# Layer norm with residual: 16-row loads and stores as two transfers of 64 partitions

## The chip, the cores and the metric

The kernel runs on one core of one Trainium2 chip. The metric is the device time of one execution in microseconds (us), lower is better. The kernel before takes 243.0 us (median of 3 runs, 242.81 to 243.03).

For one core, a run is called slow when it is more than 1.5% above the fastest run of the same kernel. Ratios below are the mean time of one kernel's fast runs over the mean of the fast runs of the other kernel in the same rounds, so they are not quite the ratio of the medians quoted beside them.

## The reference

```python
batch, seq, dim = 16, 1024, 512          # x and residual: float32, 33.6 MB each
z = x + residual
mean = np.mean(z, axis=-1, keepdims=True)
var = np.var(z, axis=-1, keepdims=True)
return gamma * (z - mean) / np.sqrt(var + eps) + beta
```

It is a stream: 67.1 MB come in, 33.6 MB go out, and each element sees little arithmetic. The whole kernel is a question of how 100.7 MB are moved.

## The kernel before

The 16384 rows are taken as 128 rows for each of 128 partitions. A block is 16 rows a partition, and 16 rows of one partition lie together in device memory (32 KB). Loads take 8 rows at a time (16 KB a partition, 2 MB in all), stores 16 rows (32 KB a partition, 4 MB). All of them go down one queue from SyncE, over 128 partitions.

```python
BLOCK = 16
X_CHUNKS = [8] * 15 + [4, 4]
R_CHUNKS = [8] * 15 + [4, 4]
OUT_CHUNKS = [16] * 7 + [8, 4, 4]
Z_ROWS = 64        # x, z and the result share this ring: 64 rows
R_ROWS = 32        # ring for the residual: 32 rows
STORE_LAG = 40     # a store is asked for 40 rows after its rows were
# ...
    def load_x(lo, n):
        nc.sync.dma_start(out=part(zbuf, Z_ROWS, lo, n), in_=dram(xf, lo, n))

    def load_r(lo, n):
        nc.sync.dma_start(out=part(rbuf, R_ROWS, lo, n), in_=dram(rf, lo, n))

    def store(lo, n):
        nc.sync.dma_start(out=dram(of, lo, n), in_=part(zbuf, Z_ROWS, lo, n))
# ... add (GpSimd), statistics (ScalarE), two affine steps (VectorE) ...
    for lo, n in spans(X_CHUNKS):
        asked = lo + n
        load_x(lo, n)                    # waits until the ring's old rows are stored
        while loads_r and loads_r[0][0] + loads_r[0][1] <= asked:
            # ... compute until the ring's old rows are added
            load_r(*loads_r.pop(0))
        store_due()                      # stores whose last row is <= asked - STORE_LAG
```

Of the kernel before, what the change touches and what calls it, by code (L numbers as in the profile page):

```python
# [12 lines left out]
BLOCK = 16  # L13


X_CHUNKS = [8] * 15 + [4, 4]
R_CHUNKS = [8] * 15 + [4, 4]
OUT_CHUNKS = [16] * 7 + [8, 4, 4]

GROUP = 4  # L20
# [1 line left out]
Z_ROWS = 64  # L22
R_ROWS = 32
# [5 lines left out]
def kernel(  # L29
# [9 lines left out]
    nc = tc.nc  # L39
    P = nc.NUM_PARTITIONS  # L40
    xf = x.flatten_outer_dims()
    rf = residual.flatten_outer_dims()
    of = out.flatten_outer_dims()
# [4 lines left out]
    def spans(sizes):  # L48

        assert sum(sizes) == total  # L50
        return [(sum(sizes[:c]), n) for c, n in enumerate(sizes)]
# [3 lines left out]
    def dram(t, lo, n):  # L55

        k = lo % BLOCK
        assert k + n <= BLOCK
        v = t[P * (lo - k) : P * (lo - k + BLOCK), :].rearrange("(p j) d -> p j d", p=P)
        return v[:, k : k + n, :].rearrange("p a b -> p (a b)")  # L60
# [15 lines left out]
    zbuf = consts.tile([P, Z_ROWS, D], FP32)  # L76
    rbuf = consts.tile([P, R_ROWS, D], FP32)

    def part(buf, size, lo, n):
        assert lo % size + n <= size  # L80
        return buf[:, lo % size : lo % size + n, :].rearrange("p a b -> p (a b)")

    def load_x(lo, n):
        nc.sync.dma_start(out=part(zbuf, Z_ROWS, lo, n), in_=dram(xf, lo, n))  # L84

    def load_r(lo, n):
        nc.sync.dma_start(out=part(rbuf, R_ROWS, lo, n), in_=dram(rf, lo, n))  # L87

    def store(lo, n):
        nc.sync.dma_start(out=dram(of, lo, n), in_=part(zbuf, Z_ROWS, lo, n))  # L90

    def zrow(j):
        return zbuf[:, j % Z_ROWS, :]
# [16 lines left out]
    groups = []  # L110
    for lo, n in spans(R_CHUNKS):
        for j in range(0, n, GROUP):
# [92 lines left out]
    added = done = asked = 0  # L205
    loads_r = spans(R_CHUNKS)
    stores = spans(OUT_CHUNKS)

    def store_due():
        nonlocal added, done  # L210
        while stores and (
            stores[0][0] + stores[0][1] <= asked - STORE_LAG or asked == total
        ):
            lo, n = stores.pop(0)
            while done < lo + n:
                added, done = next(steps)
            store(lo, n)

    for lo, n in spans(X_CHUNKS):
        asked = lo + n  # L220
        assert not stores or stores[0][0] >= asked - Z_ROWS
        load_x(lo, n)
        while loads_r and loads_r[0][0] + loads_r[0][1] <= asked:

            while added < loads_r[0][0] + loads_r[0][1] - R_ROWS:
                added, done = next(steps)
            load_r(*loads_r.pop(0))
        if lo == 0:
            spread()
        store_due()  # L230
# [35 lines left out]
```

## Time and profile before

| what | before |
|---|---|
| time | 243.0 us |
| span of the profile | 241.3 us |
| share of the data queue in the span of 16 engines | 97.9% |
| VectorE, ScalarE, GpSimd busy | 178.5, 180.1, 144.3 us |
| transfers | 44 |

From the page of the kernel before: the span, the busy share of the DMA engines in tenths and their rate in 40 slices, the data queue (packets, MB, share), the residual add on GpSimd, and the issues (KB each, median us from issue to landing).

```profile
span 241.3 us, 1109 instructions
...
DMA  7999999999999999999999999999999999999992
GB/s 261 434 435 434 434 430 418 421 425 432 432 470 436 391 426 421 429 434 426 430 434 437 430 424 429 429 451 410 425 426 432 475 387 418 462 434 432 413 410 117
DMA packets 6349, 100.74 MB, mean 417 GB/s; under 512 B 706, under 2 KB 706, under 8 KB 708
...
q1 hardware_dynamic: 6336, 100.67, 97.9%
...
L120 POOL TENSOR_TENSOR zbuf<-zbuf,rbuf 128x2048 f32<-128x2048 f32 x32 | 144.1, 4526 | 70.6 <-DMA rbuf<-in_residual_dram 69.6
...
zbuf<-in_x_dram SPq DMA_DIRECT2D x15, 2048.0 KB, 29.2
...
out_dram<-zbuf SPq DMA_DIRECT2D x7, 4096.0 KB, 28.6
```

The engines that move data are busy in every slice but the first and the last, and the rate stands at about 430 GB/s. No compute engine is busy for more than three quarters of the span. The kernel is bound by its transfers.

The small packets (706 under 512 B) are read here as completion records: 16 for each of 44 transfers, and one each for gamma and beta, make 706. Sixteen records are taken to mean that a transfer was spread over all 16 engines, which goes with the DMA share of 1.02 of 16 engines in both stretches below.

Two stretches from the windows view of the same trace. The columns are the stretch, its length, the busy time of PE, PEld, DVE, ACT and POOL (with counts), the clock, the DMA share and GB/s.

```profile
5.00:13.00 8.00, 2.07 (x2) 0.50 (x2) 0.00 (x0) 0.00 (x0) 0.02 (x1) 1.00 1.02 434
60.00:80.00 20.00, 0.00 (x0) 0.00 (x0) 19.86 (x34) 19.87 (x61) 17.95 (x5) 1.00 1.02 437
```

The trace also holds every packet with its start and its duration. A 16 KB packet takes 612 ns and a 32 KB packet 1213 ns (medians). That is 26.8 and 27.0 GB/s for each engine, and 16 such engines make about 430 GB/s.

### The profile page before, as it was taken

The page shows a single profiled execution, that of the slowest core. Times are in us where ns is not written, and L with a number is a line of the kernel's source. Part 1 is how long each engine was busy: PE and PEld are TensorE (multiplying, and loading weights), DVE is VectorE, ACT ScalarE, POOL GpSimd, SP SyncE. Part 2 cuts the span into 40 slices and gives each one's busy share as a digit, 9 for nine tenths or more (in the row PEclk, how much of TensorE's full clock was granted, in tenths as well). Part 3 has the DMA queues.
Part 4 walks back from the last instruction along what each step waited for, and adds up shares of the span by engine and source line. Part 5 has one row for each costly group of instructions (what it writes and reads, how often), then busy time and mean ns, then how long its engine had stood idle before and what let it go on. Part 6 is the DMA issues. An engine that isn't in the chain of part 4 may idle for free.

```text
span 241.3 us, 1109 instructions
## 1 busy us (share of the span) xinstructions
PE 4.1 (2%) x4; PEld 1.0 (0%) x4; DVE 178.5 (74%) x290; ACT 180.1 (75%) x546; POOL 144.3 (60%) x36
## 2 busy tenths in 40 slices
PE   3300000000000000000000000000000000000000
PEld 0000000000000000000000000000000000000000
DVE  0005999999999999899934999359991699969200
ACT  2009999999999999999709997099961999697000
POOL 0088988989889507894078940889209891860000
DMA  7999999999999999999999999999999999999992
GB/s 261 434 435 434 434 430 418 421 425 432 432 470 436 391 426 421 429 434 426 430 434 437 430 424 429 429 451 410 425 426 432 475 387 418 462 434 432 413 410 117
DMA packets 6349, 100.74 MB, mean 417 GB/s; under 512 B 706, under 2 KB 706, under 8 KB 708
## 3 DMA queue, kind: packets, MB, share of 16 engines
q1 hardware_dynamic: 6336, 100.67, 97.9%
q14 instruction: 9, 0.07, 0.1%
q10 hardware_dynamic: 4, 0.00, 0.0%
HBM read 67.11 MB, written 33.55 MB: 417 GB/s over the span
## 4 chain that ended last, share of the span: by engine, by line
DMA 62%; ACT 16%; DVE 6%; POOL 6%; SPq 1%; issue 1%; DVEq 0%; POOLq 0%
DMA rbuf<-in_residual_dram 34%; DMA out_dram<-zbuf 28%; ACT junk L131 9%; ACT junk L140 7%; POOL zbuf L120 6%; DVE zbuf L175 3%; DVE zbuf L161 3%; SPq L84 1%; ACT std L148 0%; SPq L87 0%; SPq L90 0%; DVEq L261 0%; DVE rstd L173 0%; POOLq L120 0%; DVEq L161 0%
## 5 line engine op out<-in xcount | busy, mean ns | idle before, releaser
L120 POOL TENSOR_TENSOR zbuf<-zbuf,rbuf 128x2048 f32<-128x2048 f32 x32 | 144.1, 4526 | 70.6 <-DMA rbuf<-in_residual_dram 69.6
L161 DVE SCALAR_TENSOR_TENSOR zbuf<-zbuf,nm,gamma_t 128x512 f32<-128x512 f32 x128 | 89.5, 746 | 44.4 <-issue 22.5
L131 ACT ACTIVATE junk<-zbuf 128x512 f32<-128x512 f32 x128 | 74.2, 580 | 38.9 <-POOL zbuf L120 38.9
L175 DVE SCALAR_TENSOR_TENSOR zbuf<-zbuf,rstd,beta_t 128x512 f32<-128x512 f32 x128 | 87.1, 743 | 1.2
L140 ACT ACTIVATE junk<-zbuf,nm 128x512 f32<-128x512 f32 x128 | 85.9, 671 | 0.0
L140 ACT ACTIVATION_READ_ACCUMULATOR junk<-zbuf,nm 128x1 f32 x128 | 24.0, 187 | 0.0
L131 ACT ACTIVATION_READ_ACCUMULATOR junk<-zbuf 128x1 f32 x128 | 23.9, 187 | 0.0
L148 ACT ACTIVATE std<-ssq,eps_t 128x4 f32<-128x4 f32 x32 | 8.5, 267 | 1.0
L173 DVE RECIPROCAL rstd<-std 128x4 f32<-128x4 f32 x32 | 5.6, 175 | 0.0
L186 ACT ACT_TABLE_LOAD x1 | 1.3, 1283 | 1.5 <-PEq L247 1.5
L190 PE MATMUL beta_t<-gb_row,ones 1*128 1x512 f32 x2 | 2.1, 1136 | 2.3 <-DMA gb_row<-in_beta_dram 2.3
L190 PE MATMUL gamma_t<-gb_row,ones 1*128 1x512 f32 x2 | 2.0, 1122 | 2.3 <-DMA gb_row<-in_gamma_dram 2.3
L104 DVE MEMSET ones<- 1x128 f32 x1 | 0.2, 165 | 0.8 <-PEq L247 0.8
L190 PEld LDWEIGHTS beta_t<-gb_row,ones 1*128 1x128 f32 x2 | 0.5, 308 | 3.9 <-DMA gb_row<-in_beta_dram 3.9
L190 PEld LDWEIGHTS gamma_t<-gb_row,ones 1*128 1x128 f32 x2 | 0.5, 308 | 2.2 <-issue 2.2
L247 POOL MEMSET const-float32-0.0<- 128x1 f32 x1 | 0.1, 99 | 0.2 <-issue 0.2
L186 ACT ACTIVATE warm<-eps_t 128x1 f32<-128x1 f32 x1 | 0.2, 203 | 0.0
L247 POOL MEMSET const-bfloat16-1.0<- 128x1 bf16 x1 | 0.1, 102 | 0.0
L247 POOL MEMSET const-uint8-127<- 128x1 uint8 x1 | 0.1, 102 | 0.0
L247 POOL MEMSET const-float32-1.0<- 128x1 f32 x1 | 0.1, 99 | 0.0
L106 DVE MEMSET eps_t<- 128x1 f32 x1 | 0.1, 59 | 0.0
## 6 DMA issues: line engine op xcount, KB each, us to landing
zbuf<-in_x_dram SPq DMA_DIRECT2D x15, 2048.0 KB, 29.2
rbuf<-in_residual_dram SPq DMA_DIRECT2D x15, 2048.0 KB, 29.9
out_dram<-zbuf SPq DMA_DIRECT2D x7, 4096.0 KB, 28.6
zbuf<-in_x_dram SPq DMA_DIRECT2D x2, 1024.0 KB, 32.3
rbuf<-in_residual_dram SPq DMA_DIRECT2D x2, 1024.0 KB, 32.3
out_dram<-zbuf SPq DMA_DIRECT2D x1, 2048.0 KB, 23.5
out_dram<-zbuf SPq DMA_DIRECT2D x2, 1024.0 KB, 16.7
gb_row<-in_gamma_dram ACTq DMA_DIRECT2D x1, 2.0 KB
```

The source lines that it names most:

```text
L84: nc.sync.dma_start(out=part(zbuf, Z_ROWS, lo, n), in_=dram(xf, lo, n))
L104: nc.vector.memset(ones, 1.0)
L120: nc.gpsimd.tensor_tensor(out=z, in0=z, in1=part(rbuf, R_ROWS, j0, n), op=ALU.add)
L131: nc.scalar.activation(out=junk, in_=zrow(j0 + k), func=ACT.Identity, scale=-inv_d, accum_out=nm[:, k : k + 1],)
L140: nc.scalar.activation(out=junk, in_=zrow(j0 + k), func=ACT.Square, bias=nm[:, k : k + 1], accum_out=ssq[:, k : k + 1],)
L148: nc.scalar.activation(out=std[:, :n], in_=ssq[:, :n], func=ACT.Sqrt, bias=eps_t[:, 0:1], scale=inv_d,)
L161: nc.vector.scalar_tensor_tensor(out=zrow(j0 + k), in0=zrow(j0 + k), scalar=nm[:, k : k + 1], in1=gamma_t, op0=ALU.add, op1=ALU.mult,)
L173: nc.vector.reciprocal(out=rstd[:, :n], in_=STD.pop(g)[:, :n])
L175: nc.vector.scalar_tensor_tensor(out=zrow(j0 + k), in0=zrow(j0 + k), scalar=rstd[:, k : k + 1], in1=beta_t, op0=ALU.mult, op1=ALU.add,)
L186: nc.scalar.activation(out=warm, in_=eps_t, func=ACT.Sqrt)
L190: nc.tensor.matmul(dest, ones, gb_row[:, k, :], start=True, stop=True)
L247: nc = _bacc.Bacc("TRN2", target_bir_lowering=False, num_devices=1)
```

## The change

The intent is to give loads the 32 KB descriptors that stores have, without making one transfer larger than 2 MB: 16 rows are moved as two transfers, of partitions 0 to 63 and of 64 to 127. Stores of 16 rows are cut the same way. Only the first two and the last three residual loads and the last three stores keep 128 partitions.

```diff
-X_CHUNKS = [8] * 15 + [4, 4]
-R_CHUNKS = [8] * 15 + [4, 4]
+X_CHUNKS = [16] * 8
+R_CHUNKS = [8, 8] + [16] * 6 + [8, 4, 4]
 OUT_CHUNKS = [16] * 7 + [8, 4, 4]
@@
+    def transfer(out, in_, n):
+        parts = 2 if n == BLOCK else 1
+        for h in range(parts):
+            p0, p1 = h * P // parts, (h + 1) * P // parts
+            nc.sync.dma_start(out=out[p0:p1, :], in_=in_[p0:p1, :])
+
     def load_x(lo, n):
-        nc.sync.dma_start(out=part(zbuf, Z_ROWS, lo, n), in_=dram(xf, lo, n))
+        transfer(part(zbuf, Z_ROWS, lo, n), dram(xf, lo, n), n)
@@ (load_r and store alike)
```

21 chunks of 16 rows (8 of x, 6 of the residual, 7 of the result) of 4.19 MB each are cut: 88.1 of the 100.7 MB.

More of the change, by code (lines that the diff above doesn't have):

```diff
@@ L81, in part @@
         return buf[:, lo % size : lo % size + n, :].rearrange("p a b -> p (a b)")
+    def transfer(out, in_, n):
[3 more added lines that the diff above has]
+            nc.sync.dma_start(out=out[p0:p1, :], in_=in_[p0:p1, :])
     def load_x(lo, n):
-        nc.sync.dma_start(out=part(zbuf, Z_ROWS, lo, n), in_=dram(xf, lo, n))
+        transfer(part(zbuf, Z_ROWS, lo, n), dram(xf, lo, n), n)
     def load_r(lo, n):
-        nc.sync.dma_start(out=part(rbuf, R_ROWS, lo, n), in_=dram(rf, lo, n))
+        transfer(part(rbuf, R_ROWS, lo, n), dram(rf, lo, n), n)
     def store(lo, n):
-        nc.sync.dma_start(out=dram(of, lo, n), in_=part(zbuf, Z_ROWS, lo, n))
+        transfer(dram(of, lo, n), part(zbuf, Z_ROWS, lo, n), n)
     def zrow(j):
```

## The prediction

> **What bounds the kernel now.** The transfers. The page's line of queues gives the one data queue 97.9% of the 16 engines' span; the windows show 426 to 437 GB/s in nearly every stretch of 20 us from 20 us on, with gaps only at the start and in the last 5 us. POOL (144.3 us busy), DVE (178.5) and ACT (180.1) all have slack in a span of 241.3 us. The kernel moves 100.7 MB; at the best stretches' 437 GB/s that alone is 230 us. So under 5% could be won even by perfect transfers.
>
> **What the change could win.** Loads go from 16 KB to 32 KB a descriptor. In the trace's packet records a 16 KB packet takes 611 ns and a 32 KB one (today's stores) 1213, so two small ones cost 9 ns more than a large one. 58.7 MB of loads change size: 1792 large packets, 9 ns each, over 16 engines, is about 1 us (estimate). That is all: 0.4%.
>
> **What it adds.** Transfers rise from 44 to 50. The first add needs 6 MB instead of 4 (an estimated 5 us later; the compute slack absorbs it). Each round now queues x, r and store, and the next x load waits for the store just queued; but its first half waits only for the first half of the store, with about 4.8 us of the second half (2 MB at 430 GB/s) queued behind[...]. I expect no gap from this, and no wait for compute.
>
> **What I expect to decide it.** 88 MB of the 100.7 MB now go in transfers that touch 64 partitions.[...] No run here shows it yet: every data transfer before has 128 partitions. Both halves go down one queue, in order, on all 16 engines[...]. Estimate: [...]the other 12.6 MB at 430 is 29, start and end 5: 440 us. All of the addition lies on the critical path, as transfers are the bound. Engines drift apart, though: in the trace the 16 landings of one transfer spread over 0.3 us at the start and about 3 us after halfway.[...] I say 415 us.[...]
>
> **Chances.** Faster by over 2%: 0.01. Within 2%: 0.18[...]. Slower by over 2%: 0.81.
>
> **What would show each step.** Right: in the windows, 210 to 280 GB/s while half transfers run and 430 while 128-partition ones do, with the engines' busy share still near 100%; packets of 32 KB taking 2.0 to 2.4 us; long waits of POOL for the residual, and SP waiting longer for stores.[...] Wrong on the queue: DMA share falling below 0.9 in the slices after each store, with packets still at 1.2 us; that would be a few per cent slower only.
>
> **What would make it wrong.** Engines assigned by partition, so that the halves run side by side on 8 engines each[...].

The sum of the estimate came to 440 us: to the 29 and 5 us that stand in it belongs a term for the 88 MB in halves; its rate came from no run. From the 440 the forecast takes 25 us, for a part of the loss that was expected to come back as engines drift apart (it was a guess), and so says 415. The rates and packet times named as signs of being right are forecasts. The sign of being wrong on the main step was 430 GB/s throughout and 32 KB packets of 1.2 us, as in the kernel before.

## The result and the profile after

The changed kernel takes 422.6 us (median of 4 runs, 417.83 to 425.88), against 243.01 for the kernel before in the same comparison. The ratio is 1.733, with a 95% interval of 1.718 to 1.747; the run of 425.88 us counts as slow and is left out of it. All results below are correct unless said otherwise; none was wrong.

The same lines of the page, for the changed kernel:

```profile
span 420.9 us, 1105 instructions
...
DMA  9999999999999999999999999999999999999994
GB/s 200 199 371 237 216 218 206 199 209 222 212 206 200 212 305 249 206 218 215 302 277 203 213 218 308 255 202 202 209 311 255 209 193 399 268 237 260 269 310 174
DMA packets 4525, 100.74 MB, mean 239 GB/s; under 512 B 802, under 2 KB 802, under 8 KB 804
...
q1 hardware_dynamic: 4512, 100.67, 97.8%
...
L126 POOL TENSOR_TENSOR zbuf<-zbuf,rbuf 128x2048 f32<-128x2048 f32 x32 | 143.5, 4515 | 228.3 <-DMA rbuf<-in_residual_dram 228.3
...
zbuf<-in_x_dram SPq DMA_DIRECT2D x16, 2048.0 KB, 21.9
...
out_dram<-zbuf SPq DMA_DIRECT2D x15, 2048.0 KB, 50.2
```

This is the reading to learn from. The busy share of the engines is the same (97.8% against 97.9%), and the bytes are the same, but the rate has halved: about 200 to 220 GB/s in most slices. So the engines are not idle, and nothing starves them. Each packet takes about twice as long (2558 ns against 1213 for 32 KB, see below). Busy share alone would have shown nothing. The third slice, at 371 GB/s, is where the two residual loads that kept 128 partitions run. The add on GpSimd takes what it took (4515 ns against 4526), but it waits 228.3 us for the residual instead of 69.6.

The same stretches of the windows view, changed kernel:

```profile
5.00:13.00 8.00, 2.07 (x2) 0.49 (x2) 0.00 (x0) 0.00 (x0) 0.00 (x0) 1.00 0.98 205
60.00:80.00 20.00, 0.00 (x0) 0.00 (x0) 0.00 (x0) 1.15 (x4) 5.68 (x2) 1.00 1.01 210
```

From the packet records: the 128 packets of 32 KB that start between 60 and 80 us have a median of 2558 ns. Before, packets of 32 KB took 1213. The ratio is 2.11. All 802 small packets are accounted for by 50 transfers of 16 records, and two: by the reading above, each half was still spread over all 16 engines.

### The profile page after: what moved, and what is told of

Read it like the earlier page. It is cut to its first block, busy times and chain, and to the rows that moved or that the text cites. A ratio compares the mean times of both kernels' runs of the same rounds, so it can differ in the third digit from the quotient of the medians.

```text
span 420.9 us, 1105 instructions
## 1 busy us (share of the span) xinstructions
PE 4.1 (1%) x4; PEld 1.0 (0%) x4; DVE 178.5 (42%) x290; ACT 180.3 (43%) x546; POOL 143.7 (34%) x36
## 3 DMA queue, kind: packets, MB, share of 16 engines
q1 hardware_dynamic: 4512, 100.67, 97.8%
## 4 chain that ended last, share of the span: by engine, by line
DMA 42%; another core or an unknown queue 28%; POOL 10%; DVE 6%; POOLq 2%; issue 2%; SPq 2%; DVEq 0%
DMA rbuf<-in_residual_dram 21%; DMA out_dram<-zbuf 21%; POOL zbuf L126 10%; DVE zbuf L167 3%; DVE zbuf L181 2%; POOLq L267 2%; SPq L87 2%; DVEq L267 0%; DVE rstd L179 0%; POOLq L126 0%
## 5 line engine op out<-in xcount | busy, mean ns | idle before, releaser
L126 POOL TENSOR_TENSOR zbuf<-zbuf,rbuf 128x2048 f32<-128x2048 f32 x32 | 143.5, 4515 | 228.3 <-DMA rbuf<-in_residual_dram 228.3
```

The lines of the kernel that those rows point to most:

```text
L126: nc.gpsimd.tensor_tensor(out=z, in0=z, in1=part(rbuf, R_ROWS, j0, n), op=ALU.add)
```

## The experiments

The theory: the place of a transfer's partitions decides. A transfer of lower partitions alone, or of upper ones alone, is slow; one that takes as many partitions from below 64 as from above is not. The traces do not even name the engine of a packet, so no run here shows why the place should count. The runs can only show whether it does. In the expectations below, the forecast that stands first is the theory's, and the others are the rivals' or those of a second case.

Rivals: the larger chunks and descriptors, or their order in the queue, are what costs; any transfer of few partitions is slow, whichever they are; the cost is one for each transfer.

### One transfer of 128 partitions again

```diff
-        parts = 2 if n == BLOCK else 1
+        parts = 1
```

> The changed kernel with its chunks and 32 KB descriptors kept and only the cut into 64 partitions undone (each 16-row transfer is one of 128 partitions, 4 MB). [...]32 KB packets fall back to about 1.21 us, the windows to about 430 GB/s and the time to 245 to 258 us; what is left over 243 is a gap in each of about four rounds, since the next x load now waits for the whole store with nothing queued behind it[...]. Rival (the 16-row chunks, the 32 KB descriptors or the order of the queue cost the time): about 420 us.

Measured: 256.5 us (256.09 to 257.88), ratio to before 1.056 (1.053 to 1.059). The page's lines:

```profile
DMA  8999999999999959999699995999978999999996
GB/s 299 404 435 433 458 439 412 422 458 434 412 422 407 444 191 443 412 391 433 248 412 470 355 417 242 412 412 417 403 335 330 422 413 400 417 453 444 413 402 263
...
q1 hardware_dynamic: 4176, 100.67, 94.9%
```

The rate is back, and 32 KB packets take 1213 ns. So the 16-row chunks and the 32 KB descriptors are not to blame; the cut into halves is. What is left, 13 us, looks quite different: dips in the busy share, to 5 or 6 tenths in three slices and to 7 or 8 in two more. That is a queue that runs dry, and the two later runs with an earlier store test it.

### The halves alone, with the kernel's own chunks

```diff
 X_CHUNKS = [8] * 15 + [4, 4]             # as before the change
 R_CHUNKS = [8] * 15 + [4, 4]
-        parts = 2 if n == BLOCK else 1
+        parts = 2 if n >= 8 else 1
```

> The kernel before with its own chunks (loads of 8 rows, 16 KB descriptors), and only the cut added: every transfer of 8 rows or more becomes two of 64 partitions. [...]380 to 440 us, 16 KB packets about 1.25 us instead of 0.61. Rival (32 KB descriptors or 16-row chunks): about 243 us, a little more for the added transfers.

Measured: 392.8 us (median; 381.85 to 395.8). Three of its four runs count as slow, because they lie over 1.5% above its fastest one, so no ratio is given; its one fast run is 381.85, also the profiled one. The first and the later slices differ:

```profile
GB/s 178 216 216 209 214 215 216 207 216 214 214 210 217 215 269 286 245 248 271 343 297 263 253 303 405 250 235 264 385 333 260 243 367 388 373 417 383 292 191 84
```

With 16 KB descriptors and 8-row chunks, the cut alone brings the rate to about 215 GB/s. That settles the rival of size and order from the other side. 16 KB packets that start between 100 and 140 us take about 1.26 us, against 0.61. After about 130 us the rate rises; more on this below.

### The cut at other partitions

```diff
-        parts = 2 if n == BLOCK else 1
-        for h in range(parts):
-            p0, p1 = h * P // parts, (h + 1) * P // parts
+        cuts = [0, 32, 96, 128] if n == BLOCK else [0, P]
+        for p0, p1 in zip(cuts, cuts[1:]):
```

> The changed kernel with each 16-row transfer cut at partitions 32 and 96 instead of 64: three transfers of partitions 0 to 31, 32 to 95, 96 to 127. The middle one again has 64 partitions, 2 MB and 32 KB descriptors[...]. [...]the middle transfers run at full rate and the outer two at half, so 32 KB packets form two groups, about 1.21 us and about 2.5 us, each near half of them, and the time is 315 to 350 us. Rival (any transfer of 64 partitions or fewer is slow, whichever they are, or slow in proportion to the partitions): 420 us or more.

Measured: 348.7 us over all six runs (344.9 to 362.43); the three fast ones lie between 344.9 and 346.3, ratio 1.421 (1.417 to 1.425), inside the expectation. The profiled run (351.2) is one that counts as slow.

In its packet records, 45% of the 32 KB packets take under 1.3 us, and 27% between 2.3 and 2.7 us; the rest lies between or above. So the two groups are there, but not near half of the packets each, as expected. The first chunk of x shows the reason in order. Partitions 0 to 31 give each engine two packets; the second ones, 16 in all, take 2.56 to 2.59 us. Partitions 32 to 95 follow with four for each engine; after the first of them, which overlaps the end of the transfer ahead, the other 48 take 1.21 to 1.23 us. Partitions 96 to 127 are next, at 2.10 to 2.52 us for their first packets. So a transfer of 64 partitions, 2 MB and 32 KB descriptors runs at full rate when it lies across partition 64, between two of 32 partitions that do not.

### Even and odd partitions

```diff
-            p0, p1 = h * P // parts, (h + 1) * P // parts
-            nc.sync.dma_start(out=out[p0:p1, :], in_=in_[p0:p1, :])
+            nc.sync.dma_start(out=out[h::parts, :], in_=in_[h::parts, :])
```

> The changed kernel with its two transfers taken as the even and the odd partitions instead of the lower and the upper 64: as many partitions, bytes, descriptors and transfers[...]. [...]clearly faster than 423 us; about 243 to 250[...], and 300 to 400[...]. Rival (64 partitions in one transfer are slow, whichever they are): 410 to 430 us.

The two ranges are two cases; what told them apart was a guess.

Measured: 245.8 us (245.43 to 246.54), ratio 1.011 (1.009 to 1.013). The page's lines:

```profile
GB/s 258 428 426 431 428 428 435 444 439 446 434 444 428 365 434 423 428 391 428 434 387 434 376 450 402 391 434 386 430 423 375 412 408 466 428 428 431 412 419 197
DMA packets 4525, 100.74 MB, mean 412 GB/s; under 512 B 802, under 2 KB 802, under 8 KB 804
```

This is the cleanest of the tests. The number of packets, the number of transfers (802 small packets, as after the change), the bytes, the descriptors and the order of the queue are those of the changed kernel. Only the choice of which 64 partitions go together differs, and 423 us become 246. With it differs where the bytes lie in device memory: a half is one stretch of 2 MB, the even partitions are every second 32 KB. That this is the cause is excluded by the middle transfers of the run before, which are one stretch of 2 MB too and ran at full rate. Neither the number of partitions nor the number of transfers costs the time; their place does.

### 32 and 16 partitions

```diff
-        parts = 2 if n == BLOCK else 1
+        parts = 4 if n == BLOCK else 1      # second run: 8
```

> The changed kernel with four transfers of 32 partitions each instead of two of 64. [...]the time stays at 400 to 450 us. Rival (rate in proportion to the number of partitions of a transfer): about 600 to 800 us. Rival (cost per transfer): 37 more halves cost as much again over before, about 600 us.

> The changed kernel with eight transfers of 16 partitions each[...]. [...]32 KB packets of about 4.9 us while in step, and 600 to 850 us[...]. Rival (the limit is 8 engines' worth for any transfer of fewer than 128 partitions): about 420 us, as with 64 and 32.

Quarters: 419.6 us (414.92 to 425.84), ratio 1.719 (1.708 to 1.731), as with halves, though there are 92 transfers instead of 50 (the expectation's 37 more should be 42). Eighths: 561.4 us (median of six, 554.59 to 579.13; three of them count as slow), ratio of the fast ones 2.289. The eighths missed the expected 600 to 850 us. The start of the run is as expected and the later part is not; its rates in slices of 14.2 us (the profiled run is of the slow ones, 571.1 us):

```profile
GB/s 115 127 181 264 120 113 113 111 111 111 127 124 115 113 111 111 111 122 207 216 206 210 305 215 168 177 205 263 177 166 170 275 193 158 353 211 258 177 199 273
```

Until about 256 us the rate is 111 to 127 GB/s in all slices but those of the whole residual loads. The packets there (60 to 140 us) take 4528 ns, 3.73 times 1213. The windows view has 113 GB/s for this run from 100 to 120 us, and 210 GB/s from 60 to 80 us both for quarters and for halves, so 32 partitions in a row go like 64. After that, with loads and stores alternating, the rate is mostly 160 to 275, and the time falls short of the forecast for that reason. What brings this about is taken up below.

| partitions of a transfer | 32 KB packet, 60 to 140 us | over 1213 ns |
|---|---|---|
| 128 (before, stores) | 1213 ns | 1.00 |
| 64, even or odd | 1213 ns | 1.00 |
| 64, lower or upper | 2558 ns | 2.11 |
| 32, in a row | 2551 ns | 2.10 |
| 16, in a row | 4528 ns | 3.73 |

### Loads alone, stores alone

```diff
-    def transfer(out, in_, n):
-        parts = 2 if n == BLOCK else 1
+    def transfer(out, in_, n, split=2):
+        parts = split if n == BLOCK else 1
@@ first run: stores uncut; second run: both loads uncut
-        transfer(dram(of, lo, n), part(zbuf, Z_ROWS, lo, n), n)
+        transfer(dram(of, lo, n), part(zbuf, Z_ROWS, lo, n), n, 1)
```

In both expectations the first figure is for loads and stores that are limited alike.

> The changed kernel with only its loads cut at partition 64; stores of 16 rows go in one transfer of 128 partitions. 58.7 of the 88.1 MB stay cut. The change cost 180 us for 88.1 MB, 2.04 us a MB. [...]243 + 120 = 363 us, and some 12 us for the gaps that the run with whole transfers showed (the next x load waits for the whole store again), so 355 to 385. If stores were spared[...], all the loss is in the loads: about 423 us.

> The changed kernel with only its stores cut at partition 64 (29.4 MB); loads of 16 rows go in one transfer of 128 partitions. [...]243 + 60 = 303 us and some 12 us of gaps, so 295 to 325, with 32 KB packets of about 2.4 us in the store-only tail. If stores are spared: 243 to 258 us and all 32 KB packets near 1.21 us.

Loads cut: 395.9 us (395.25 to 396.05), ratio 1.628, above the 355 to 385 expected and below the 423 of the rival. Stores cut: 307.4 us (306.73 to 308.32), ratio 1.264, as expected. The rates, loads cut:

```profile
GB/s 190 207 336 286 210 211 213 213 213 214 213 210 207 201 203 310 270 210 203 213 227 361 213 214 213 213 373 213 213 213 207 290 296 193 217 447 426 428 425 325
```

and the stretch of stores near the end, stores cut:

```profile
245.00:280.00 35.00, 0.00 (x0) 0.00 (x0) 18.92 (x31) 15.60 (x49) 6.60 (x2) 1.00 1.00 241
```

Both directions are limited, stores not all the time. With only the loads cut, the final stores run at 425 to 447 GB/s; with only the stores cut, the same kind of stretch runs at 241. Both runs have whole transfers on one side and so the dry queue of the first experiment, so they are set against its 256.5 us: the loads cost 139.4 us for 58.7 MB (2.37 us a MB) and the stores 50.9 us for 29.4 MB (1.73 us a MB). At 205 GB/s throughout, the cost would be 2.55 us a MB (1 MB at 205 GB/s against 430). The loads pay nearly all of it, the stores two thirds. My expected figure for the loads had spread the loss evenly over all bytes, and that was the error. Where the stores save their third can be seen in the packet records of the run with only the stores cut: of its second pair of store halves, the 64 packets that start from 120 to 126 us have a median of 1213 ns, and the 64 from 126 to 136 us one of 2547. The first half of a pair that follows loads is spared, the second is not; the third and fourth pair show the same (medians of 1213 to 1276 and of 2547).

### Engines out of step

In the changed kernel the rate rises from 200 to 220 to between 302 and 311 in one slice of each of four rounds after 150 us. The prediction said that part of the loss would come back, because engines drift apart. The completion records of a transfer (16, read as one for each engine) show how far apart the engines are. Spread between the first and the last, in us:

```
                          until 150 us    later                    GB/s later
before                    0.3 to 2.5      up to 3.3                about 430, no halves
changed                   0.7 to 1.3      2.8 to 11.0 from 165 us  200 to 310
only loads cut            0.6 to 1.2      0.4 to 1.3               203 to 214 while loading
8-row chunks, cut         0.8 to 1.6      up to 22.6               235 to 417
```

While loads go in halves at about 210 GB/s, the spread hardly grows for 150 us (0.7 to 1.3 us), less even than before the change (0.3 to 2.5). It jumps when stores and loads begin to alternate. Where it stays small (only loads cut), nothing comes back, but there the stores are whole, so that no cut store is left to recover anything; where it grows largest, most comes back. That goes with the idea that engines out of step lose less. It is a correlation over four runs, not a test, and nothing here shows how it would come about. A second idea fits as well: that loads and stores slow each other less than loads slow loads; that is not tested either. In the run of 8-row chunks, the first store packets, from 139 us on, took as little as 1.21 us, and the rate rose before the spread did.

The packets of the changed kernel show where most of the time comes back, and neither idea covers it. Of the 2688 packets of 32 KB, 396 take less than 1.3 us. None of these starts before 150 us. 286 of them lie in four clusters of 65 to 80, one for each round, and the first half of a store has 64 packets. The first cluster is the clearest. The queue is taken in the order of the issues, as the sizes of the packets show; here the last load packet ends at 153.4 us, and the next load is asked for at 158.8. The 48 packets that start from 153.5 to 157.1 us are all of the store's first half, out of partitions 0 to 63. They take 1213 to 1232 ns, with the completions just before only 1.3 us apart, no load in flight and no engine in the other half yet. Those of the second half that start from 159.3 to 164.6 us take 2546 to 2565 ns. The windows view shows loads, first half and second half in turn (a packet counts where it starts):

```profile
145.00:150.00 5.00, 0.00 (x0) 0.00 (x0) 0.00 (x0) 0.00 (x0) 0.00 (x0) 1.00 1.02 210
154.00:157.00 3.00, 0.00 (x0) 0.00 (x0) 0.00 (x0) 0.00 (x0) 2.65 (x1) 1.00 1.01 437
160.00:164.00 4.00, 0.00 (x0) 0.00 (x0) 1.77 (x3) 4.00 (x13) 4.00 (x2) 1.00 0.92 188
```

In the run of quarters the same stretches of the first store have 437 and 205 GB/s, although two quarters lie in the first and two in the second. So it is about the first four store packets of each engine after a run of loads that are spared, not a certain transfer. Why is open. By an estimate, 396 packets that are 1345 ns shorter make 33 us over 16 engines.

Two runs were to be the test: a copy of 1 MB ahead of everything, to hold 8 of the 16 engines back by half a transfer. Each expectation gives two cases, first that the rate rises and then that it does not; which engines would have to be apart for it was a guess.

```diff
+    late = P * (total - BLOCK)               # rows that the last stores write again
+    nc.sync.dma_start(
+        out=of[late : late + 512, :].rearrange("(p a) d -> p (a d)", p=8),
+        in_=xf[late : late + 512, :].rearrange("(p a) d -> p (a d)", p=8))
```

> The changed kernel with one more transfer ahead of all others: 1 MB copied within device memory in 8 rows of 128 KB[...] (the rows that it writes are overwritten by the final stores, so the result stays right).[...] Theory of the partly recovered loss:[...] the windows show well over 300 GB/s from the start until the first load that waits for a store, at about 80 us, and the total falls to 300 to 390 us. [...]no such rise, and 423 us plus the 5 us of the copy.

Measured: 427.3 us (421.33 to 429.25), ratio 1.743 from the two fast runs. The copy is contiguous; it went as 16 packets of 64 KB with 16 completion records (818 small packets against 802), so it held all engines back alike. (I had expected it to go to 8 engines alone.) The run tested nothing.

```diff
+        v = t[late : late + 1024, :].rearrange("(p q a) d -> p q (a d)", p=8, q=2)
+        return v[:, 0, :]                    # every second of 16 blocks, p outermost
```

> The stagger again. The copy of the first attempt was cut into 16 pieces of 64 KB, one for each engine (16 packets of 65,536 bytes and 16 completion records), so it held all 16 back alike and tested nothing. This copy takes every second of 16 blocks, so its outer dimension stays 8: it should show 8 completion records and hold only 8 engines back by about 4.9 us. Theory of the recovery:[...] the windows show over 300 GB/s from the start to about 80 us and the total falls to 300 to 390 us. If[...] drift is not what recovers, about 425 us and 200 to 215 GB/s in those windows.

Measured: 437.6 us (436.78 to 439.96), ratio 1.801 (1.797 to 1.805). This time the copy has 8 completion records (810 small packets), and the spread is 4.2 to 6.3 us in most early transfers, as wanted. The rate did not rise, and the time is 12 us over the 425 expected for that case, which is not explained (the first line includes bytes of the copy):

```profile
5.20:8.80 3.60, 0.71 (x1) 0.00 (x0) 0.00 (x0) 0.00 (x0) 0.00 (x0) 1.00 0.86 228
9.00:13.00 4.00, 0.00 (x0) 0.00 (x0) 0.00 (x0) 0.00 (x0) 0.00 (x0) 1.00 0.99 205
60.00:80.00 20.00, 0.00 (x0) 0.00 (x0) 6.58 (x11) 3.25 (x11) 0.00 (x0) 1.00 0.99 206
```

What it did show is that the slow packets do not need all 16 engines. By the counts of packets and records, from 4.8 to about 8.8 us only the 8 engines that were not held move the first half; the other 8 are still copying. Yet their second packets (8 of them, starting between 6.66 and 7.11 us) take 2.58 to 2.60 us, as when all 16 take part (2558 ns in the changed kernel). So holding these eight back took nothing off the packets of the others, and the stagger did not do what it was made for. What brings part of the loss back stays open. (That the copy's own traffic slowed those 8 packets is not excluded by itself, and the copy's packets did grow from about 3.0 to 3.4 us beside them; but the 8 packets last what packets of halves last in the changed kernel, and the kernel before moved about 430 GB/s with packets of 1213 ns.)

### The queue that ran dry, and a version to beat both

In the run with whole transfers, the next x load waits for a store behind which nothing stands in the queue (SyncE waits for stores at its x loads 4 times, 125.5 us in all). If that is the 13 us, asking for stores one chunk earlier must take them back.

```diff
-STORE_LAG = 40
+STORE_LAG = 32
```

> The whole-transfer kernel (128 partitions, 16 rows, 32 KB descriptors) with its stores asked for one chunk earlier (the lag falls from 40 rows to 32), so that another x and residual load stand in the queue behind the store that the next x load waits for. Theory of the gaps: the 13 us that the whole-transfer run lost against the kernel before were empty queues after each store, so the time falls from 256.5 to 241 to 245 us, the transfer queue fills 97% or more of the engines' span, and at the most about 1 us is won against 243 by the larger descriptors. Rival (4 MB transfers are slower as such): it stays at 250 to 257.

> The even and odd partitions version with the same lag of 32 rows. If its 2.6 us over the kernel before are short queues, 241 to 245 us;[...] 245 to 247 as before.

(The last figure is for any other cause of the 2.6 us.)

Whole transfers with the earlier store: 243.5 us (243.01 to 243.94), ratio to before 1.0011 (0.9999 to 1.0024). Even and odd partitions with the earlier store: 244.0 us (243.22 to 244.34), ratio 1.003 (1.0017 to 1.0044), so most of their 2.6 us were short queues. The lines of the first, to be set beside those of the run with whole transfers:

```profile
DMA  7999999999999999999999999999999999999964
GB/s 261 434 431 437 434 434 435 434 434 435 401 434 434 435 428 434 434 434 428 434 434 428 430 428 430 434 428 428 434 434 435 434 412 412 450 434 434 418 285 184
...
q1 hardware_dynamic: 4176, 100.67, 97.4%
```

The dips are gone, so the dry queue is shown: 13.0 us over the four x loads that wait for a store, 3.3 us each. Neither version beats the kernel before. The windows of the trace give 430 GB/s for the kernel before and 431 for this one between 20 and 228 us, and what follows is 13.3 us before and 13.7 here. The 1 us that larger descriptors were estimated to save is too small to appear.

## Why the prediction was right

- **The bound.** Right. The transfers filled 97.9% of the engines' span before and 97.8% after, and the time followed their rate.
- **The gain of larger descriptors, about 1 us.** Of the right order, that is, nothing: with 32 KB descriptors, whole transfers and a full queue the time is 243.5 against 243.15.
- **No gap from the new order of the queue.** Right for the changed kernel, whose first half waits for the first half of the store only; the engines stayed busy (97.8%). Undoing the cut took that away and cost 13 us. A gap was 3.3 us.
- **Half transfers.** Right that they are slow, and the step that decided it; the ground given for it is not shown by any run. The cut alone makes the kernel slow (halves of 8-row chunks, 382 us in the fast run), undoing it alone makes it fast (256.5 us), and the even or the odd 64 partitions run at full rate (246 us) in the same number of equal transfers. So it is the place of the partitions. One thing this does not cover: the first store packets after a run of loads (437 GB/s out of 64 partitions).
- **The size.** 415 was predicted and 422.6 measured, from two errors that nearly cancel. A packet of a half takes 2.11 times as long, and the rate is 205 to 210 GB/s, less than the forecast reckoned with; 88.1 MB would be 430 us at 205, and with the 29 and 5 us of the prediction the whole 464 us instead of 440. More came back than thought: 41 us of that, instead of 25. That 415 came so close is in part luck.
- **Drift.** The weakest step: part of the loss did come back, but the reason given does not hold where it can be seen best. It was said that engines drift apart and that this brings part of the loss back. In fact the spread stayed near 1 us for 150 us of loads, most of them in halves, and most of what came back, an estimated 33 of 41 us, came in short packets that cluster at the first half of each store; in the first of these clusters no engine was in the other half and no load was in flight. The cause of these is open, and no run excludes that drift does the rest.
- **Stores.** The run with only the stores cut excludes the branch in which reads of SBUF are spared throughout (307.4 us, not about 243). They are spared in part, in the first half of a store after loads.

## What to carry to other kernels

It was the place of the partitions that counted when a transfer was cut. Pieces along the free dimension, with all 128 partitions, kept about 430 GB/s (16 KB packets of 612 ns); so did the even and the odd partitions (245.8 us for the whole kernel), and partitions 32 to 95 kept packets of 1.21 to 1.23 us. The lower and the upper 64 did not (2558 ns), nor did 32 or 16 in a row (2551 and 4528 ns). Two halves that together cover all partitions did not make up for it when one queue took them in turn (422.6 us against 243.0). On another kernel, read it from the packets before relying on it. And read the rate beside the busy share: engines that were 98% busy at half the rate were here the sign that each packet took twice as long, and the fix was not in the queue.
